# A hybrid attention layer on one core: row scales by PE transposes, x split in pairs, dilated loads one unit ahead

## The chip, the core and the metric

The kernel runs on one core of a Trainium2 chip. TensorE (PE) multiplies matrices into PSUM, whose eight banks per partition all are in use here; VectorE (DVE), ScalarE (ACT) and GpSimd (POOL) work on tiles in SBUF; the queue of SyncE (SP) issues every DMA of this program. Each engine and the queue run their instructions in the order in which the program has them: an instruction that waits holds up all behind it. The metric is the device time in microseconds, the median of several runs.

## What is computed

One decoder layer on x (2048 rows of 1024): an RMSNorm, one input projection, two attention mixers with eight heads of 64 each, a SiLU gate on each, an output projection, and x added. Cut to what matters:

```python
hdn = rmsnorm(x, norm_gain)
q_a, k_a, v_a, g_a, q_b, k_b, v_b, g_b = split(hdn @ w_in)
q_a = rope(rmsnorm(q_a, q_norm_a), pos)      # k_a, q_b, k_b likewise, per head
o_a = banded_attention(q_a, k_a, v_a, 127, sinks) * silu(g_a)
o_b = dilated_attention(q_b, k_b, v_b) * silu(g_b)   # windows (128,1), (512,4), (2048,16)
x = x + concat([o_a, o_b]) @ w_out
```

Mixer A sees 128 keys back and shares each key head among four query heads. Mixer B merges three patterns, weighted by their softmax denominators.

## The kernel before

All matrices are float32. To keep their precision, a factor is split into a high part (`xh`, `wh`, rounded to the PE's format) and the rest (`xl`, `wl`), and every product is three matmuls (`mm3`, L238): high by high, high by low, low by high. `x_split` makes the parts of x: ACT copies `xh` (L154), POOL or DVE subtracts (L156).

The work is cut into eight stages: four B stages (two heads of mixer B each), two A stages (four heads of mixer A each) and two output stages O (half of the output columns each). A stage walks over four blocks `sb` of 512 rows, a block over two halves `hf` of 256 rows. `proj` does a half: two tiles of 128 rows for q, k and v (24 matmuls of 384 columns each), then one gate (B) or two (A) of 24 matmuls with 256 columns, transposed, so that a row's scale lies along the free axis there. The RMSNorm of x isn't applied to x but afterwards: `rst` holds 1/rms of each row as a column (for v and q, k), and `RB` holds half of it as a row, the same in all 128 partitions, for the gate (L317). In the first stage `squares` and `rstd` work the row sums out: for the first two halves from x with a matmul against ones (L198), for the others from `xn`, a second copy of x in row order (L204, L205). `rstd` writes the scales to DRAM as single values (`rsr<-rss`, L213), and every half of every B and A stage loads them back in a broadcast (`RB<-rsr`, L270).

`norm_rope` and `norm_split` make the heads' norm and rotation: POOL raises the mean square to the power -1/2 (`fac`, L182), DVE multiplies (L433), ACT and POOL split (L442 to L445); `qk_transposes` turns the result by PE, through the PSUM bank `tq`. Results of the attention's second product (PV) go through the bank `po`. Both names have one bank; `pj`, `sc` and `pt` have two each.

The attention is cut into units of four steps (scores, transposes, PV, after). Units of the window pattern follow in the same stage (`units_B`, `units_A`); the dilated patterns need all rows, so q, k and v of a B stage are spilled to DRAM and `units_D` loads them again in the stage after it (`cq`, `ck`, `cl`, `cv`). `advance` does one step between two chunks of the projection, as far as a running sum of estimated costs allows; up to three units are in flight. `final` (A) and the end of `after` (D) load a row of softmax factors in a broadcast (`Rb`, one buffer) and multiply on POOL. At the end the Tile framework's scheduler sets the order on each engine and puts in the waits. The profile calls buffers by the names in the code; `in_` marks an input.

Of the kernel before, what the change touches and what calls it, by code (L numbers as in the profile page):

```python
# [21 lines left out]
XB = 3  # L22
# [10 lines left out]
def hybrid_layer(ctx, tc, xT, xn, x, wB, wA, wO, ng, gains, sinks, rot, masks, ident, out):  # L33
# [57 lines left out]
    rs_row = [dram([512], f"rsr{sb}") for sb in range(4)]  # L91
# [58 lines left out]
    def x_split(si, hf, g):  # L150
        f = XS.pop((si, hf, g))
        h = xp.tile([128, 4, 256], F32R, name="xh", bufs=3)
        l = xp.tile([128, 4, 256], F32R, name="xl", bufs=XB)
        nc.scalar.activation(h, f, AF.Copy)  # L154
        eng = nc.gpsimd if g == 0 or hf >= 6 else nc.vector
        eng.tensor_tensor(l, f, f32(h), op=OP.subtract)  # L156
        XG[si, hf, g] = (h, l)
        if si == 0 and hf < 2:
            squares(f, g)

    def first_half():
        for g in range(2):
            f = xp.tile([128, 4, 256], F32, name="xs")
            h = xp.tile([128, 4, 256], F32R, name="xh", bufs=3)
            l = xp.tile([128, 4, 256], F32R, name="xl", bufs=XB)
            for c in range(4):
                nc.sync.dma_start(f[:, c], xT[0][:, 4 * g + c, :])
                W[0][2](4 * g + c, lambda: (nc.scalar.activation(h[:, c], f[:, c], AF.Copy),
                                            nc.vector.tensor_tensor(l[:, c], f[:, c], f32(h[:, c]), op=OP.subtract)))
            XG[0, 0, g] = (h, l)  # L170
            XS[0, 0, g] = f
        for g in range(2):
            squares(XS.pop((0, 0, g)), g)
# [10 lines left out]
    def squares(f, g):  # L184
        sq = wk.tile([128, 4, 256], F32, name="P")
        if g == 0:
            SQ.append(wk.tile([128, 2, 256], F32, name="o1c", bufs=1))
        nc.scalar.activation(sq, f, AF.Square)
        nc.vector.tensor_tensor(sq[:, 0:2], sq[:, 0:2], sq[:, 2:4], op=OP.add)
        nc.vector.tensor_tensor(SQ[-1][:, g], sq[:, 0], sq[:, 1], op=OP.add)  # L190

    def rstd(i0, n):
        ss = wk.tile([128, 4], F32, name="rss")[:, :n]
        if i0 < 4:
            p = ps.tile([128, 2], F32, name="tq")
            for t in range(2):
                for g in range(2):
                    nc.tensor.matmul(p[:, t:t + 1], SQ[-1][:, g, 128 * t:128 * t + 128], one, start=g == 0, stop=g == 1,  # L198
                                     skip_group_check=True)
        else:  # L200
            p = ss
            for i in range(n):
# [794 lines left out]
```

## Time and profile before

| | |
|---|---|
| median of 3 runs | 1323.74 us (1321.75 to 1323.76) |
| profiled execution: its time, and its span from first to last instruction | 1318.66 us, 1316.9 us |
| mean granted clock of TensorE in it | 0.949 |
| busy: PE, DVE, ACT, POOL | 1189.3, 877.2, 821.3, 657.0 us |
| moved by DMA | 228.31 MB, 173 GB/s on average |

The profile is of one execution. A row of a group gives the line, engine and operation, output and inputs, the count, then the busy time, the mean of one instruction in ns, and the idle time just before these instructions with what ended it. "PEclk" is the share of TensorE's full clock that was granted. Matmuls overlap one another, so the mean duration of one is longer than the distance from one to the next. A wait row reads: engine, its output and line, what it waited for, then us in total, times, and the longest.

### The profile page before, as it was taken

The numbers are of one execution on the slowest core, as the hardware profiler recorded it, in microseconds if no ns is written. First come the engines' busy times: TensorE is split into PE (matmuls) and PEld (weight loads), VectorE is DVE, ScalarE is ACT, GpSimd is POOL, SyncE is SP. The second block draws the span as 40 slices with busy tenths as digits, with TensorE's granted clock in tenths as the row PEclk, the third lists the DMA queues.
The fourth block names the chain that finished last, engine by engine and source line by source line (L and its number), as shares of the span: only waits on it lengthen the run. The fifth ranks groups of instructions, "written<-read, shape, count | busy, mean of one in ns | idle before, by whom it ended". The sixth has DMA issues, their size and how long they took to land.

```text
span 1316.9 us, 25065 instructions
## 1 busy us (share of the span) xinstructions
PE 1189.3 (90%) x8264; PEld 1153.3 (88%) x8264; DVE 877.2 (67%) x2280; ACT 821.3 (62%) x2280; POOL 657.0 (50%) x706
## 2 busy tenths in 40 slices
PE   7587788989999899798988999998799989999899
PEld 6586788989889798797988898998799979999898
DVE  6344476867977688766877788898688878632221
ACT  5446567867867687676766776787567757522210
POOL 5564544366553655545565446574445563233122
PEclk8798989989989899998999999999899999999999
DMA  8366578877768776786856864544333214556462
GB/s 253 101 178 170 150 226 202 229 208 200 201 193 252 203 212 179 187 243 183 223 151 211 213 179 147 156 137 141 108 98 97 93 54 142 183 185 214 156 192 89
DMA packets 195729, 228.31 MB, mean 173 GB/s; under 512 B 28560, under 2 KB 140944, under 8 KB 195600
## 3 DMA queue, kind: packets, MB, share of 16 engines
q1 hardware_dynamic: 195600, 226.71, 59.6%
q8 instruction: 66, 1.08, 0.4%
q14 instruction: 63, 0.52, 0.1%
HBM read 171.78 MB, written 54.86 MB: 172 GB/s over the span
## 4 chain that ended last, share of the span: by engine, by line
PE 50%; DMA 20%; DVE 13%; ACT 7%; POOL 4%; issue 4%; SPq 1%; POOLq 0%; DVEq 0%; ACTq 0%
PE pj L238 35%; DMA rsr<-rss 3%; DVE G L322 3%; DVE t L433 2%; PE po L830 2%; DMA Rb<-rD 2%; DMA stg<-in_wB 2%; DMA xs<-in_xT 2%; PE po L629 2%; DMA stg<-in_wO 2%; POOL fac L182 1%; PE pt L703 1%; PE sc L574 1%; PE po L719 1%; DMA stg<-in_wA 1%
## 5 line engine op out<-in xcount | busy, mean ns | idle before, releaser
L238 PE MATMUL pj<-wh,xh 128*128 128x384 f32 (+1 forms) x1008 | 339.4, 338 | 32.4 <-DVE gz L317 23.5
L238 PE MATMUL pj<-wh,xl 128*128 128x384 f32 (+1 forms) x1008 | 338.0, 337 | 7.4 <-DVE xl L156 7.4
L238 PE MATMUL pj<-wl,xh 128*128 128x384 f32 (+1 forms) x1008 | 339.0, 336 | 0.0
L156 POOL TENSOR_TENSOR xl<-xs,xh 128x1024 fp32r<-128x1024 f32 x79 | 191.7, 2429 | 164.1 <-ACT xh L154 163.9
L238 PEld LDWEIGHTS pj<-wh,xh 128*128 128x128 f32 x1008 | 197.2, 196 | 36.5 <-DVE gz L317 25.5
L154 ACT ACTIVATE xh<-xs 128x1024 fp32r<-128x1024 f32 x126 | 133.0, 1056 | 152.7 <-PE pj L238 99.7
L238 PEld LDWEIGHTS pj<-wh,xl 128*128 128x128 f32 x1008 | 197.6, 196 | 9.2 <-DVE xl L156 8.2
L238 PEld LDWEIGHTS pj<-wl,xh 128*128 128x128 f32 x1008 | 197.4, 196 | 1.6 <-DVE wl L104 0.4
L558 DVE TENSOR_TENSOR ptl<-pt,pth 128x512 fp32r<-128x512 f32 (+3 forms) x232 | 141.3, 618 | 31.0 <-ACT pth L557 28.4
L238 PE MATMUL pj<-xh,wgh 128*128 128x256 f32 x496 | 147.4, 297 | 5.1 <-DVE V L300 4.8
L557 ACT ACTIVATE pth<-pt 128x512 fp32r<-128x512 f32 (+3 forms) x232 | 123.0, 543 | 40.4 <-PE pt L816 11.3
L238 PE MATMUL pj<-xh,wgl 128*128 128x256 f32 x496 | 145.1, 292 | 0.0
L238 PE MATMUL pj<-xl,wgh 128*128 128x256 f32 x496 | 145.0, 292 | 0.0
L420 POOL TENSOR_TENSOR t<-t,t 128x256 f32<-128x256 f32 (+1 forms) x96 | 77.4, 806 | 69.7 <-DVE t L411 41.3
L322 DVE SCALAR_TENSOR_TENSOR G<-gz 128x128 f32<-128x128 f32 x128 | 95.3, 783 | 24.1 <-ACT gz L319 23.6
L433 DVE TENSOR_TENSOR t<-t,fac 128x256 f32<-128x256 f32 (+1 forms) x96 | 79.4, 845 | 39.6 <-POOL fac L182 36.9
L238 PEld LDWEIGHTS pj<-xh,wgh 128*128 128x128 f32 x496 | 98.3, 198 | 6.8 <-ACT wh L103 3.4
L238 PEld LDWEIGHTS pj<-xl,wgh 128*128 128x128 f32 x496 | 98.1, 198 | 0.4
L238 PEld LDWEIGHTS pj<-xh,wgl 128*128 128x128 f32 x496 | 98.1, 198 | 0.2
L795 ACT ACTIVATE P<-P,scD 128x256 f32<-128x256 f32 (+3 forms) x128 | 71.6, 561 | 30.9 <-DVE scD L794 29.9
L182 POOL TENSOR_TENSOR fac<-un,mhalf 128x8 f32<-128x8 f32 (+1 forms) x48 | 85.1, 1773 | 2.3
L444 POOL TENSOR_TENSOR hl<-t,hl 128x128 fp32r<-128x128 f32 (+1 forms) x96 | 62.1, 647 | 47.7 <-ACT hl L442 47.6
(185 smaller groups left out, 3064.4 us busy)
## 6 DMA issues: line engine op xcount, KB each, us to landing
xs<-in_xT SPq DMA_DIRECT2D x94, 512.0 KB
xs<-mx SPq DMA_DIRECT2D x32, 512.0 KB
vd<-V SPq DMA_DIRECT2D x64, 128.0 KB
qd<-Q SPq DMA_DIRECT2D x32, 256.0 KB
TT<-tab SPq DMA_DIRECT2D x32, 256.0 KB
cv<-vd SPq DMA_DIRECT2D x32, 256.0 KB
cq<-qd SPq DMA_DIRECT2D x32, 256.0 KB
ck<-kd SPq DMA_DIRECT2D x64, 128.0 KB
```

Of the source, the lines that this page charges most:

```text
L154: nc.scalar.activation(h, f, AF.Copy)
L156: eng.tensor_tensor(l, f, f32(h), op=OP.subtract)
L182: nc.gpsimd.tensor_tensor(y, u, mhalf.to_broadcast([128, n]), op=OP.pow)
L238: nc.tensor.matmul(o, a, b, start=first and n == 0, stop=last and n == 2, skip_group_check=True)
L322: nc.vector.scalar_tensor_tensor(G[si, sb][gc][:, :, 2 * half + j, :], e[:, js].rearrange("p (r u) -> p r u", r=4), 1.0, z[:, js].rearrang ...
L420: nc.gpsimd.tensor_tensor(t1[:, :n], t1[:, :n], t2[:, :n], op=OP.add)
L433: nc.vector.tensor_tensor(t1v, t1v, fac[:, tt, :, None].to_broadcast([128, nh, 64]), op=OP.mult)
L444: nc.gpsimd.tensor_tensor(lo, t1v[:, :nq], f32(hi), op=OP.subtract)
L557: nc.scalar.activation(hi, pt, AF.Copy)
L558: nc.vector.tensor_tensor(lo, pt, f32(hi), op=OP.subtract)
L629: nc.tensor.matmul(po[:, o:o + 256], a, b, start=n_ == 0, stop=n_ == len(seq) - 1, skip_group_check=True)
L795: nc.scalar.activation(pd, pd, AF.Exp, bias=nb, scale=-1.0, accum_out=l)
```

## The change

It has six parts.

1. The row scales of stage one: `rstd` is called for every half, one half ahead, from the loaded x; `xn` isn't read any more. `rb_make` transposes `rst`, spread over 128 columns, on PE, and ACT copies the result to `RB`. One row of it is written to DRAM for the later stages, which load it a half ahead (`rb_load`).
2. `xh` and `xl` are tiles of two chunks instead of four, six buffers each; the third and fourth pair are split in the middle of the last gate.
3. The gate writes its first product into `G` itself, and forms the result there in one instruction instead of two. The rope table is loaded into its place `TT` and multiplied there.
4. `norm_factors` (POOL) comes before the gate's matmuls and `norm_split` after the gate; the transposes of a half (`deferred`) come in the second tile of the next half instead of the first.
5. The loads of a dilated unit are a step of their own, issued when the unit before it starts. The last products of A and D are put into a list `late`, each due after a number of unit steps, and their loads are issued two or three steps before.
6. `tq` and `po` become one name with two buffers; `Q` and its copy `qc` have two buffers each.

The places where the order moves. First SP's queue in stage one, around the third and fourth half: before, the scales' writes (L213), the broadcasts (L270), and tables and x behind them.

```order
L213 DMA rsr_93<-rss 128x2x1
L304 DMA vd_326<-V 4x32x256
L270 DMA RB<-rsr_93 128x256
L304 DMA vd_326<-V 4x32x256
L147 DMA xs<-in_xT 128x1024
L213 DMA rsr_94<-rss 128x4x1
L270 DMA RB<-rsr_94 128x256
L388 DMA tab_2_476<-TT 128x512
L382 DMA gz<-in_rot 128x256
```

And now (`xs` is x, `tab` the rope tables kept for later stages, `vd` the spilled v):

```order
L392 DMA TT<-in_rot 128x4x64
L214 DMA rsr_93<-RB 1x256
L398 DMA tab_1_321<-TT 128x512
L148 DMA xs<-in_xT 128x1024
L398 DMA tab_2_503<-TT 128x512
L314 DMA vd_350<-V 4x32x256
L214 DMA rsr_94<-RB 1x256
```

No load of this stage waits for a write of the scales any more; the writes that are left stand for stage two. Next DVE in the fourth B stage, fourth half, around the gate's first product (L317, now L331); `t` is the rotated q and k, `xl` the low part of x, `ptl` that of the probabilities. Before:

```order
L156 TENSOR_TENSOR xl<-xs,xh 128x1024
L433 TENSOR_TENSOR t_7998<-t_7998,fac 128x256
L558 TENSOR_TENSOR ptl<-pt,pth 128x384
L433 TENSOR_TENSOR t_8035<-t_8035,fac 128x256
L317 TENSOR_TENSOR gz<-pj,RB 128x256
L558 TENSOR_TENSOR ptl<-pt,pth 128x512
L322 SCALAR_TENSOR_TENSOR G<-gz 128x4x32 x2
```

And now:

```order
L157 TENSOR_TENSOR xl<-xs,xh 128x512 x2
L331 TENSOR_TENSOR G<-pj,RB 128x2x4x32
L446 TENSOR_TENSOR t_8241<-t_8241,fac 128x256
L446 TENSOR_TENSOR t_8303<-t_8303,fac 128x256
L335 SCALAR_TENSOR_TENSOR G<-gz,G 128x4x64
```

The products with `fac` have moved from ahead of the gate's first product to behind it. Last POOL at the same place; `osum`, `o1c` and `Rb` belong to the end of a dilated unit. Before:

```order
L874 TENSOR_TENSOR osum<-osum,Rb 128x512
L875 TENSOR_TENSOR o1c<-o1c,Rb 128x512
L428 TENSOR_TENSOR un<-un,eps_84 128x8
L420 TENSOR_TENSOR t_8035<-t_8035,t_8036 128x256
L876 TENSOR_TENSOR osum<-osum,o1c 128x512
L182 TENSOR_TENSOR fac<-un,mhalf 128x8
```

And now:

```order
L899 TENSOR_TENSOR o1c<-o1c,Rb 128x512
L478 CAST qc<-Q 128x8x32
L457 TENSOR_TENSOR hl<-t_7874,hl 128x128
L430 TENSOR_TENSOR t_8241<-t_8241,t_8242 128x256
L458 TENSOR_TENSOR hl<-t_7874,hl 128x128
L457 TENSOR_TENSOR hl<-t_7965,hl 128x128
L458 TENSOR_TENSOR hl<-t_7965,hl 128x128
L904 TENSOR_TENSOR osum<-osum,Rb 128x512
L436 TENSOR_TENSOR un<-un,eps_84 128x8
L905 TENSOR_TENSOR osum<-osum,o1c 128x512
L430 TENSOR_TENSOR t_8303<-t_8303,t_8304 128x256
L182 TENSOR_TENSOR fac<-un,mhalf 128x8
```

The two products with `Rb`, which stood side by side ahead of `fac`, are apart by six other instructions.

The diff, cut to its core:

```diff
-XB = 3
+XB = 6
+QB = {"Q": 2, "qc": 2}
...
-    rs_row = [dram([512], f"rsr{sb}") for sb in range(4)]
+    rs_row = [dram([256], f"rsr{hf}") for hf in range(8)]
...
     def x_split(si, hf, g):
-        f = XS.pop((si, hf, g))
-        h = xp.tile([128, 4, 256], F32R, name="xh", bufs=3)
-        l = xp.tile([128, 4, 256], F32R, name="xl", bufs=XB)
+        f = XS[si, hf, g // 2][:, 2 * (g % 2):2 * (g % 2) + 2]
+        h = xp.tile([128, 2, 256], F32R, name="xh", bufs=XB)
+        l = xp.tile([128, 2, 256], F32R, name="xl", bufs=XB)
         nc.scalar.activation(h, f, AF.Copy)
-        eng = nc.gpsimd if g == 0 or hf >= 6 else nc.vector
+        eng = nc.gpsimd if g < 2 or hf >= 6 else nc.vector
         eng.tensor_tensor(l, f, f32(h), op=OP.subtract)
...
-    def rstd(i0, n):
-        ss = wk.tile([128, 4], F32, name="rss")[:, :n]
-        if i0 < 4:
...
-        else:
-            for i in range(n):
-                t = wk.tile([128, 1024], F32, name="P") if i0 == 4 else xp.tile([128, 1024], F32, name="xs")
-                nc.sync.dma_start(t, xn[(i0 + i) * 128:(i0 + i + 1) * 128, :])
-                nc.scalar.activation(t, t, AF.Square, accum_out=ss[:, i:i + 1])
...
-            nc.sync.dma_start(rs_row[i0 // 4][128 * (i0 % 4):128 * (i0 % 4 + n)].rearrange("(i p) -> p i", p=128), ss)
+    def rb_make(hf):
+        p = ps.tile([128, 2, 128], F32, name="po", bufs=2)
+        for t in range(2):
+            nc.tensor.transpose(p[:, t], rst[:, 2 * hf + t:2 * hf + t + 1].to_broadcast([128, 128]), idf)
+        RBS[0, hf] = wk.tile([128, 256], F32, name="RB")
+        nc.scalar.activation(RBS[0, hf], p.rearrange("p t e -> p (t e)"), AF.Copy, scale=0.5)
+        nc.sync.dma_start(rs_row[hf][None, :], RBS[0, hf][0:1, :])
+
+    def rb_load(si, hf):
+        if si > 0 and STAGES[si][0] != "O":
+            RBS[si, hf] = wk.tile([128, 256], F32, name="RB")
+            nc.sync.dma_start(RBS[si, hf], bcast_row(rs_row[hf], 0, 256))
...
                 if tt == 0 and nx:
-                    x_load(*nx, 0)
                     x_load(*nx, 1)
                     x_split(*nx, 0)
+                    x_split(*nx, 1)
                     if si == hf == 0:
                         late_constants(1)
+                        rb_make(0)
                     rope_tables(*nx)
-                    if si == 0 and sb < 3 and half == 1:
-                        rstd(4 * sb + 4, 4)
-                if tt == 0:
+                    if si == 0 and hf < 7:
+                        for g in range(2):
+                            squares(XS[nx + (g,)], g)
+                    rb_load(*nx)
+                if tt == 1:
+                    if si == 0 and hf < 7:
+                        rstd(hf + 1)
                     while deferred:
                         yield from deferred.pop(0)()
...
-            hls = norm_split(kind, nq, nk, sb, half, t1s, un)
+            fac = norm_factors(nh, sb, half, un)
+            RB = RBS.pop((si, hf))
             for gc in range(ngc):
...
+                    if nx and gc == ngc - 1 and c in (1, 3):
+                        x_split(*nx, 2 + c // 2)
                     yield 330
-                z = wk.tile([128, 256], F32, name="gz", bufs=2)
-                nc.vector.tensor_tensor(z, pg, RB, op=OP.mult)
+                z = G[si, sb][gc][:, :, 2 * half:2 * half + 2, :]
+                nc.vector.tensor_tensor(z.rearrange("p r j u -> p j r u"), jru(pg), jru(RB), op=OP.mult)
                 nc.scalar.activation(e, z, AF.Tanh)
-                for j in range(2):
-                    js = slice(128 * j, 128 * j + 128)
-                    nc.vector.scalar_tensor_tensor(G[si, sb][gc][:, :, 2 * half + j, :],
-                                                   e[:, js].rearrange("p (r u) -> p r u", r=4), 1.0,
-                                                   z[:, js].rearrange("p (r u) -> p r u", r=4), op0=OP.add, op1=OP.mult)
+                nc.vector.scalar_tensor_tensor(z, e, 1.0, z, op0=OP.add, op1=OP.mult)
-            if nx:
-                x_split(*nx, 1)
-                if si == hf == 0:
-                    rstd(2, 2)
+            hls = norm_split(kind, nq, nk, t1s, fac)
+            if si == 0 and hf < 7:
+                rb_make(hf + 1)
...
-                pt = ps.tile([128, 4, 128], F32R, name="tq")
+                pt = ps.tile([128, 4, 128], F32R, name="po", bufs=2)
...
         def after():
             rows(p)
-            final(p)
+            late.append([5, lambda: final(p)])
...
+                def first():
+                    rb = bcast(0)
+                    late.append([3, lambda: second(rb)])
+
+                def second(rb):
+                    nc.gpsimd.tensor_tensor(o1, o1, rb, op=OP.mult)
+                    rb = bcast(1)
+                    late.append([3, lambda: third(rb)])
...
     def advance():
+        tick()
         if not todo:
             if pending:
+                for unit in pending[:2]:
+                    if callable(unit[-1]):
+                        unit.pop()()
                 pipe.append([pending.pop(0), 0])
```

`tick` counts every entry of `late` down by one and runs those that are due.

More of the change, by code (lines that the diff above doesn't have):

```diff
@@ new lines, in squares, with rstd @@
+        for j in range(2):
+            nc.scalar.activation(sq[j], f[:, 2 * j:2 * j + 2], AF.Square)
+        nc.vector.tensor_tensor(sq[0], sq[0], sq[1], op=OP.add)
+        nc.vector.tensor_tensor(SQ[-1][:, g], sq[0][:, 0], sq[0][:, 1], op=OP.add)
+    def rstd(hf):
+        ss = wk.tile([128, 2], F32, name="rss")
+        p = ps.tile([128, 2], F32, name="po", bufs=2)
+        for t in range(2):
+            for g in range(2):
+                nc.tensor.matmul(p[:, t:t + 1], SQ[-1][:, g, 128 * t:128 * t + 128], one, start=g == 0, stop=g == 1,
+                                 skip_group_check=True)
+        c = slice(2 * hf, 2 * hf + 2)
@@ L256, in proj @@
             return
-        Q[si, sb] = [st.tile([128, 2, 4, 128], F32R, name="Q", bufs=3) for _ in range(nq // 2)]
-        qc = st.tile([128, 2, 4, 4, 32], F32R, name="Q", bufs=3) if kind == "B" else None
+        Q[si, sb] = [st.tile([128, 2, 4, 128], F32R, name=nm, bufs=QB[nm]) for nm in ("Q", "qc")]
         K[si, sb] = (st.tile([128, nk, 4, 5, 32], F32R, name="KK"), KLZ[(4 * si + sb) % 2])
@@ L266, in proj @@
             nx = next_half(si, hf)
-            xg = [XG.pop((si, hf, g)) for g in range(2)]
+            xg = [XG.pop((si, hf, g)) for g in range(4)]
             TC, TS = TB.pop((si, hf))
-            RB = wk.tile([128, 256], F32, name="RB", bufs=1)
-            nc.sync.dma_start(RB, bcast_row(rs_row[sb], half * 256, 256))
+            if nx:
+                x_load(*nx, 0)
             t1s = []
@@ L366, in hybrid_layer @@
     deferred = []
+    late = []
     tabs = {}
@@ L429, in norm_split @@
         rsqrt(fac.rearrange("p a h -> p (a h)"), u.rearrange("p a h -> p (a h)"), 2 * nh)
+        return fac
+    def norm_split(kind, nq, nk, t1s, fac):
+        nh = nq + nk
+        n = nh * 64
         hls = []
@@ L912, in hybrid_layer @@
     first_half()
-    rstd(0, 2)
+    rstd(0)
     late_constants(0)
@@ L924, in hybrid_layer @@
         own = {"B": 4 * 2900, "A": 4 * 2600, "O": 0}[kind] if n else 0
-        total = left + sum(c for u in pending for _, c in u) + own
+        total = left + sum(st_[1] for u in pending for st_ in u if not callable(st_)) + own
         done = pr = 0.0
```

160 lines of the change are left out of this document (81 added, 79 removed).

## The prediction

> **What bounds it now.** The page comes first.
>
> ```profile
> span 1316.9 us, 25065 instructions
> PE 1189.3 (90%) x8264; PEld 1153.3 (88%) x8264; DVE 877.2 (67%) x2280; ACT 821.3 (62%) x2280; POOL 657.0 (50%) x706
> PEclk8798989989989899998999999999899999999999
> PE 50%; DMA 20%; DVE 13%; ACT 7%; POOL 4%; issue 4%; SPq 1%; POOLq 0%; DVEq 0%; ACTq 0%
> ```
>
> TensorE (PE) is busy 1189 of 1317 us, so at most 128 us are plain idle time; the digits of its granted clock, with sevens and eights among the nines of the left half and hardly any at the right, say that more is lost by slow matmuls. Half of the chain that ended last is PE, a fifth is DMA. Where that is, a table by stage tells. The windows are the start of the second half-block of projection stage one (25 us), the starts of the stages after it (second to fourth B stage, two A stages), and the first output stage; columns are length, busy time and instructions of PE, of its weight loads, of DVE, ACT and POOL, the granted clock, DMA share and GB/s.
>
> ```profile
> 25.00:185.00 160.00, 119.45 (x708) 115.92 (x708) 71.50 (x191) 85.39 (x223) 88.46 (x119) 0.83 0.57 165
> 185.00:349.00 164.00, 155.10 (x1058) 150.45 (x1057) 125.41 (x336) 121.63 (x346) 86.70 (x101) 0.97 0.76 211
> 349.00:523.00 174.00, 160.35 (x1082) 154.91 (x1081) 131.13 (x344) 128.30 (x360) 93.43 (x107) 0.95 0.73 208
> 523.00:705.00 182.00, 164.78 (x1086) 158.63 (x1087) 132.76 (x344) 126.37 (x358) 99.66 (x112) 0.93 0.72 198
> 705.00:918.00 213.00, 197.29 (x1375) 188.26 (x1374) 179.20 (x489) 153.59 (x457) 124.14 (x134) 0.98 0.58 167
> 918.00:1106.00 188.00, 173.73 (x1224) 169.76 (x1223) 150.40 (x412) 125.67 (x383) 97.20 (x92) 0.96 0.32 96
> 1106.00:1213.00 107.00, 106.99 (x889) 106.18 (x888) 47.67 (x102) 43.45 (x97) 36.35 (x22) 1.00 0.59 184
> ```
>
> Stage one needs 160 us for 708 matmuls, 0.226 us each, with PE idle 40.6 us at a clock of 0.83. The next three B stages take 0.155, 0.161 and 0.168 us for one. The output stage at 1106 runs 889 matmuls at clock 1.00 without idle time, 0.120 us each. So stage one is the slow place, and the chain inside it names the cause:
>
> ```profile
> by line: DMA rsr<-rss 28.1%; DMA xs<-in_xn 9.4%; DMA xs<-in_xT 7.8%; issue 6.7%; DVE G L322 4.3%; DMA P<-in_xn 3.4%; PE pj L238 3.4%; DMA stg<-in_wB 2.8%; POOL fac L182 2.7%; DMA gz<-in_rot 2.5%; ACT xs L205 2.4%; DMA RB<-rsr 2.4%; POOL TT
> ...
> 38.38 5.47 DMA P<-in_xn
> ...
> 60.18 9.98 DMA rsr<-rss
> ...
> 71.10 4.02 DMA gz<-in_rot
> ```
>
> The write of the row scales to DRAM in single 4-byte values (rsr<-rss) holds 28.1% of these 160 us, 45 us in five writes, one of them 9.98 us. Loads of the second copy of x (in_xn, into xs and P) hold 12.8%, 20.5 us. The row scales come back as the broadcast RB, which the gate's first DVE product (L317) needs, and PE's accumulators come free only behind that product. PE's waits, first in stage one, then in the rest of the span:
>
> ```profile
> PE pj L238 <- DVE gz L317: 11.2, 2, 6.3
> PE tq L461 <- POOL hl L444: 9.0, 1, 9.0
> ```
>
> ```profile
> PE pj L238 <- DVE gz L317: 12.3, 6, 4.1
> PE pt L603 <- DVE ptl L558: 6.9, 2, 6.2
> PE po L629 <- DVE osum L552: 6.5, 3, 3.7
> PE sc L789 <- DMA ck<-kd: 6.0, 3, 3.4
> PE sc L574 <- ACT KK L478: 4.8, 1, 4.8
> PE pj L238 <- DVE xl L156: 4.8, 2, 4.2
> PE po L830 <- DVE ptl L558: 4.0, 1, 4.0
> PE po L629 <- DVE ptl L558: 3.9, 3, 1.7
> PE tq L470 <- ACT klz L479: 3.4, 1, 3.4
> ```
>
> These nine rows hold 52.6 us. Behind several of them stands one event, seen at 606 to 619 us on DVE and POOL (start, duration, instruction, idle time before it and its releaser):
>
> ```profile
> 612.10 1.28 POOL L875 TENSOR_TENSOR o1c<-o1c,Rb 128x512 f32<-128x512 f32 x1 [4.44 <-DMA Rb<-rD]
> 615.42 1.65 POOL L182 TENSOR_TENSOR fac<-un,mhalf 128x8 f32<-128x8 f32 x1
> ```
>
> ```profile
> 617.10 1.48 DVE L433 TENSOR_TENSOR t<-t,fac 128x256 f32<-128x256 f32 x1 [7.19 <-POOL fac L182]
> ```
>
> POOL waits 4.44 us for the broadcast Rb, so fac is computed late; DVE stands 7.19 us before L433, and the probability split that PE wants, and the gate product, queue behind it. Over the span DVE loses this much there, and POOL this much to the two Rb loads of a dilated unit:
>
> ```profile
> DVE t L433 <- POOL fac L182: 36.9, 10, 8.1
> ```
>
> ```profile
> POOL o1c L875 <- DMA Rb<-rD: 44.9, 12, 9.3
> POOL osum L874 <- DMA Rb<-rD: 33.8, 6, 11.0
> ```
>
> **The change, part by part.** *Row scales in stage one.* Removed from its chain are the five 4-byte writes, the eight RB loads of that stage and the twelve loads of in_xn. In their place stand, a half ahead, 32 half-width ACT squares for 16 full-width ones, 32 DVE additions for eight, eight pairs of PE transposes with an ACT copy each, eight 1-KB writes on SP, and 24 more of the L198 column sums. What stage one costs without the round trips I read from its neighbours, which have the same projections and no round trip on their chain: 708 matmuls at 0.155 to 0.168 us are 110 to 119 us. I take the slowest neighbour, 119, because stage one has none of the cheap transposes of dilated units in its mix: 41 us saved. The ends are 50 us (fastest neighbour) and 20 us (only the waits on gz and hl go, 11.2 + 9.0). The price of the new PE work:
>
> ```profile
> 17.43 0.73 PE L198 MATMUL tq<-one,o1c 128*128 128x1 f32 x6
> ```
>
> Six such records take 0.73 us, 0.122 each. The 24 column sums are 48 records (each is recorded twice), with 16 transposes 64 records, 7.8 us; half falls into idle time that is left, so 4 us on the path (0 to 8). The new transposes also wait at the head of PE's queue for POOL's power of the row sums, with the next projection's matmuls behind them; late by one POOL subtraction of x (2.43 us, row below) in each of eight halves that is 19 us, which the 20-us end covers. I count none, since the column sum and the transpose of a half stand some 30 projection matmuls apart, 3.6 us at 0.120. Stage one: -41 + 4 = -37 us.
>
> *x in pairs of chunks.* ACT copies 252 halves for 126 wholes, and POOL and DVE subtract twice as often at half the width:
>
> ```profile
> L154 ACT ACTIVATE xh<-xs 128x1024 fp32r<-128x1024 f32 x126 | 133.0, 1056 | 152.7 <-PE pj L238 99.7 <-DMA xs<-in_xT 36.0 <-PE pt L238 8.4
> L557 ACT ACTIVATE pth<-pt 128x512 fp32r<-128x512 f32 x144 | 84.1, 593 | 19.5 <-PE pt L703 11.3 <-PE pt L609 3.8 <-PE po L719 2.5
> L156 POOL TENSOR_TENSOR xl<-xs,xh 128x1024 fp32r<-128x1024 f32 x79 | 191.7, 2429 | 164.1 <-ACT xh L154 163.9
> L672 POOL TENSOR_TENSOR o1c<-osum,Rb 128x512 f32<-128x512 f32 x16 | 21.2, 1327 | 48.5 <-DMA Rb<-rA 38.2 <-DMA stg<-in_wO 9.7 <-POOL hl L445 0.7
> L322 DVE SCALAR_TENSOR_TENSOR G<-gz 128x128 f32<-128x128 f32 x128 | 95.3, 783 | 24.1 <-ACT gz L319 23.6
> ```
>
> By the 512-wide copy, 252 x 0.593 = 149 for 133 us on ACT; by the 512-wide POOL product, 158 x 1.327 = 210 for 192 us on POOL. That is +16 and +18 us on engines that idle 496 and 660 us, so nothing on the path by itself; the cover is that idle time, and in stage one POOL, busy 88 of 160 us, would be busy some 90 of 123. What it buys: the second half of x, before split in one piece once the gate's fourth chunk is done, is now split after its second and its fourth, which bears on the row DVE xl (4.8 us).
>
> *Gate.* Two 128-wide products become one 256-wide one: 64 instructions for 128 at 0.783 us. If one costs as much as one now, DVE saves 50 us of 877; if it costs two, nothing. It shortens the gate's tail, which no PE wait names; I count nothing.
>
> *Order of the norm.* fac is issued ahead of the gate's matmuls, and L433's products behind the gate's first product, so what waited behind L433 on DVE (gz, ptl) no longer does; in exchange the q/k transposes run one tile later, at the second projection tile of the next half, and attention units start that much later. The late list cuts POOL's final products into steps of two or three unit steps after their loads are issued, so the 78.7 us of the two Rb rows mostly go, and SP no longer stands before Rb until rD has landed. *Dilated loads* go out a unit ahead: the ck row, 6.0 us. *Shared banks:* transposes and PV take turns in two banks instead of one each: the osum row (6.5) and the KK and klz rows (8.2). Behind the dilated loads on SP's queue stand x and weight loads; they have a whole half-block of lead.
>
> All nine rows of the rest of the span are thus touched: 52.6 us is one end, and 0 the other if each wait only moves to the next item of an in-order queue. I take the middle, 26 us, nearer to neither, as the example at 617 us shows both: the wait goes, and DVE still has the same products to do.
>
> The sum: -37 - 26 = -63 us. The profiled execution took 1318.66 us with a span of 1316.9; the median of the three runs, 1323.74, is 5.1 above it. So 1255.7 for a profiled run and 1260.7 for the median; I say 1261.
>
> The clock is a reserve that this sum does not hold. In the five windows from 185 to 1106 the shares short of 1.00 times the lengths are 4.9 + 8.7 + 12.7 + 4.3 + 7.5 = 38 us. The Trainium skill, "TensorE: Matmul & The Clock Gate" (Part 1: The HAM clock gate), says that the array's clock falls to half after an idle window of about 3.4 us and comes back after a busy one. The windows agree in kind: 0.83 where PE waits 9.0 us at a time, 1.00 where it never waits. By that rule half of the waits would take half of the 38 us with them, 19 us, and the sum would be 1242.
>
> **The rivals.** *Stage one alone (1287).* The waits after 185 us move but do not shrink, 1323.74 - 37. For it: 496 us of ACT idle time and 440 of DVE did not prevent them. Against it: the event at 617 us has a named cause that goes.
>
> *Both at their good ends (1228).* Stage one at the fastest neighbour's rate (-46 with the added PE work) and the other waits nearly all gone (-50). For it: the lost clock above, which goes with the waits.
>
> *The rope tables become late (1298).* The table is now loaded straight into TT in 256-byte runs, and read and written in place by POOL. The load took 4.02 us at 71.10 in 1-KB runs; the 4-byte write at 60.18, 9.98. Nearer to the first, but if it costs the second, eight halves pay 6 us each, 48, and eat stage one's 37. It decides once load and four POOL products outlast a half (some 15 us), since the load is issued a half ahead; that speaks against it. The Trainium skill, "DMA: Bandwidth & Descriptors" (Specifications), sets 512 B as the least transfer for full rate and has shorter ones read, modified and written; by that rule this load is slower than before, and the rival gets its chance. The runs of before agree only at 4 bytes.
>
> *Slower (1343): the shared banks hold up PE.* 304 uses (96 PV, 160 q/k transposes, 48 small ones) take turns in two banks, and every use waits until the last but one is read out. A PV result is read by two instructions:
>
> ```profile
> L550 ACT ACTIVATE ob<-po 64x512 f32<-64x512 f32 x64 | 38.0, 594 | 12.0 <-PE po L629 7.0 <-PE po L830 3.1 <-ACT pth L557 0.9
> L554 DVE TENSOR_TENSOR osum<-po,ob 64x512 f32<-64x512 f32 x32 | 21.7, 680 | 2.5 <-ACT ob L550 1.8
> ```
>
> That is 0.594 + 0.680 = 1.27 us; 96 times 122 us. If half of the PV results stopped PE for that long, the gain of 63 would be gone; at two thirds, 82 us, the time is 1343. For it: transposes never stood behind PV before. Against it: with a single bank PV waited on osum just three times, 6.5 us.
>
> **How the numbers follow.** My case 0.50 (about 1240 to 1280), stage one alone 0.17, both good ends 0.17, late tables 0.08, slower 0.08. The range takes in 1225 (a little under the good ends) to 1300 (late tables); beyond lie the slower rival and some tail of the good one, 0.15 together. Faster by over 0.2%, about what a measurement of this kernel can tell from no change: 0.92; of the banks' 0.08, 0.06 is slower and 0.02 within 0.2%.
>
> **What would show it.** Right: no rsr<-rss on the chain; stage two starts near 148 us instead of 185, with a clock over 0.93 in stage one; the wait of the norm product on fac under 12 us of 36.9; POOL's waits on Rb under 25 us of 78.7. Wrong: new PE waits on po (banks), DVE waits on TT (tables), stage one past 165 us, or the rows gz and ptl at their old sums.

## The result, and the profile after

The changed kernel takes 1268.9 us in the median (1265.6 to 1271.7), the kernel before, run beside it, 1322.7: a ratio of 0.9594, 95% interval 0.9561 to 0.9627, 53.8 us less. The profiled execution has a span of 1269.9 us for 1316.9; it was the longest of its four, and that of before (1318.66 us) shorter than every run behind its median, so the profiles differ by 47.0 us where the medians differ by 53.8. The page of after, its span, busy times and granted clock:

```profile
span 1269.9 us, 25442 instructions
PE 1179.8 (93%) x8328; PEld 1143.5 (90%) x8328; DVE 867.5 (68%) x2288; ACT 837.1 (66%) x2418; POOL 685.3 (54%) x788
PEclk9899989999999899898998999999899999999999
```

The chain that ended last can't be followed back to stage one here, so that the write of the scales is off it is read from PE's waits below. PE has 64 matmuls more and is busy for 9.5 us less. The sevens and eights that stood at the start of its clock are now eights and nines. By stage (first half-block left out, then the start of each stage as before: three more B stages, two A stages, the first output stage; length, busy time and instructions of PE, its weight loads, DVE, ACT and POOL, granted clock, DMA share, GB/s):

```profile
23.00:157.00 134.00, 119.67 (x780) 116.00 (x781) 90.14 (x213) 88.45 (x247) 99.83 (x132) 0.92 0.48 139
157.00:326.00 169.00, 151.29 (x1042) 147.04 (x1040) 120.88 (x329) 123.31 (x360) 89.91 (x111) 0.98 0.74 209
326.00:501.00 175.00, 160.80 (x1073) 154.73 (x1074) 125.54 (x341) 127.56 (x373) 96.56 (x117) 0.95 0.73 205
501.00:672.00 171.00, 161.47 (x1087) 156.57 (x1085) 128.70 (x349) 128.95 (x378) 97.43 (x119) 0.95 0.74 211
672.00:871.00 199.00, 189.91 (x1346) 183.33 (x1346) 167.44 (x460) 147.04 (x446) 129.18 (x143) 0.98 0.61 176
871.00:1058.00 187.00, 179.68 (x1274) 172.53 (x1273) 147.27 (x426) 137.45 (x431) 104.11 (x105) 0.98 0.32 99
1058.00:1167.00 109.00, 107.12 (x888) 106.13 (x887) 49.40 (x106) 46.46 (x116) 38.31 (x31) 1.00 0.59 184
```

Stage two starts at 156.7 us for 185.3: 28.6 us of the 47.0 by which the span is shorter. The rest, 18.4 us, lies in the stages behind; of these the two A stages (213 and 189 us in before) now take 199 and 187. PE's waits in stage one, then in the rest (us in total, times, longest):

```profile
PE pj L244 <- DVE V L310: 4.7, 2, 4.3
PE sc L244 <- POOL xl L157: 4.5, 2, 2.3
PE po L211 <- POOL rst L182: 3.1, 2, 2.9
PE pj L244 <- ACT xh L155: 2.6, 1, 2.6
PE po L474 <- ACT RB L213: 1.1, 1, 1.1
```

```profile
PE po L474 <- POOL hl L457: 7.9, 7, 2.0
PE pj L244 <- DVE V L310: 7.2, 7, 2.5
PE po L498 <- ACT KK L477: 6.4, 2, 5.5
PE pj L244 <- ACT xh L155: 4.1, 1, 4.1
PE po L474 <- DVE osum L570: 3.7, 1, 3.7
PE pt L828 <- DVE ptl L574: 2.8, 2, 1.5
PE pt L619 <- DVE ptl L574: 2.7, 1, 2.7
PE pj L244 <- ACT wh L101: 2.2, 2, 2.0
PE po L484 <- DVE osum L740: 2.0, 1, 2.0
```

The waits on the gate's product, 11.2 and 12.3 us before, are down to 0.8 us. In stage one only small rows are left. In the rest the waits have moved to the q/k transposes (L474, L498) and to V, in smaller pieces; only one of these rows stands for the x split (ACT xh). Where the prediction expected DVE and POOL to stop waiting, they have not:

```profile
DVE t L446 <- POOL fac L182: 30.1, 13, 5.7
```

```profile
POOL o1c L899 <- DMA Rb<-rD: 55.1, 13, 7.6
POOL osum L904 <- DMA Rb<-rD: 39.7, 13, 6.7
```

DVE still waits 30.1 us on fac, and POOL waits 94.8 us for the broadcasts of a dilated unit where it waited 78.7. The costs of what was added (line, count, busy time, mean ns of one, idle time before it):

```profile
L155 ACT ACTIVATE xh<-xs 128x512 fp32r<-128x512 f32 x252 | 153.5, 627 | 115.8 <-PE pj L244 98.8 <-DMA xs<-in_xT 8.3 <-issue 4.3
L157 POOL TENSOR_TENSOR xl<-xs,xh 128x512 fp32r<-128x512 f32 x158 | 213.7, 1365 | 143.8 <-ACT xh L155 139.1 <-DMA TT<-tab 2.2
L335 DVE SCALAR_TENSOR_TENSOR G<-gz,G 128x256 f32<-128x256 f32 x64 | 47.5, 742 | 9.3 <-ACT gz L334 9.1
L198 PE MATMUL po<-one,o1c 128*128 128x1 f32 x64 | 8.7, 248 | 0.0
L211 PE MATMUL po<-idf,rst 128*128 128x128 f32 x16 | 3.4, 297 | 3.1 <-POOL rst L182 3.1
L395 POOL TENSOR_TENSOR TT<-TT,gt 128x128 f32<-128x128 f32 x64 | 35.1, 570 | 34.4 <-DMA TT<-in_rot 34.4
```

### The profile page after: what moved, and what is told of

The parts are those of the page before. It is cut to its first block, busy times and chain, and to the rows that moved or that the text cites. A ratio compares the mean times of both kernels' runs of the same rounds, so it can differ in the third digit from the quotient of the medians.

```text
span 1269.9 us, 25442 instructions
## 1 busy us (share of the span) xinstructions
PE 1179.8 (93%) x8328; PEld 1143.5 (90%) x8328; DVE 867.5 (68%) x2288; ACT 837.1 (66%) x2418; POOL 685.3 (54%) x788
## 5 line engine op out<-in xcount | busy, mean ns | idle before, releaser
L244 PE MATMUL pj<-wh,xh 128*128 128x384 f32 (+1 forms) x1008 | 334.1, 334 | 18.6 <-ACT xh L155 6.7
L244 PE MATMUL pj<-wl,xh 128*128 128x384 f32 (+1 forms) x1008 | 334.9, 332 | 1.4 <-DVE wl L102 0.8
L244 PE MATMUL pj<-wh,xl 128*128 128x384 f32 (+1 forms) x1008 | 331.9, 331 | 1.1 <-POOL xl L157 0.8
L157 POOL TENSOR_TENSOR xl<-xs,xh 128x512 fp32r<-128x512 f32 x158 | 213.7, 1365 | 143.8 <-ACT xh L155 139.1
L155 ACT ACTIVATE xh<-xs 128x512 fp32r<-128x512 f32 x252 | 153.5, 627 | 115.8 <-PE pj L244 98.8
L244 PEld LDWEIGHTS pj<-wl,xh 128*128 128x128 f32 x1008 | 194.6, 193 | 3.6 <-DVE wl L102 1.1
L244 PEld LDWEIGHTS pj<-wh,xl 128*128 128x128 f32 x1008 | 194.4, 193 | 3.5 <-DVE xl L157 1.3
L446 DVE TENSOR_TENSOR t<-t,fac 128x256 f32<-128x256 f32 (+1 forms) x96 | 76.9, 815 | 33.0 <-POOL fac L182 30.1
L814 ACT ACTIVATE P<-P,scD 128x128 f32<-128x128 f32 (+3 forms) x128 | 71.6, 560 | 40.5 <-DVE scD L813 39.6
L157 DVE TENSOR_TENSOR xl<-xs,xh 128x512 fp32r<-128x512 f32 x94 | 79.8, 859 | 20.2 <-ACT xh L155 19.8
L599 ACT ACTIVATE P<-P,scA 128x256 f32<-128x256 f32 (+1 forms) x128 | 63.1, 495 | 23.4 <-DVE scA L598 23.0
```

The costliest lines, as they stand in the source:

```text
L244: nc.tensor.matmul(o, a, b, start=first and n == 0, stop=last and n == 2, skip_group_check=True)
L446: nc.vector.tensor_tensor(t1v, t1v, fac[:, tt, :, None].to_broadcast([128, nh, 64]), op=OP.mult)
L599: nc.scalar.activation(pd, pd, AF.Exp, bias=nb[i], scale=-1.0, accum_out=l[i])
L814: nc.scalar.activation(pd, pd, AF.Exp, bias=nb, scale=-1.0, accum_out=l)
```

## The experiments

Lengths of stages are what tells most here. They are taken from the first projection matmul of a stage to that of the next; "B" is the sum of the second to fourth stage, "A" of the two A stages, "O" of the two output stages, all in the one profiled execution of the kernel. The ratio is to the runs of before on the same chip. All in us.

| kernel | median | ratio (95%) | stage one | B | A | O |
|---|---|---|---|---|---|---|
| before | 1322.7 | 1 | 179.5 | 519.4 | 401.6 | 210.6 |
| changed | 1268.9 | 0.9594 (0.9561 to 0.9627) | 151.1 | 515.7 | 386.0 | 211.6 |
| rows_only | 1289.2 | 0.9736 (0.9705 to 0.9768) | 162.5 | 528.5 | 378.5 | 210.3 |
| no_rows | 1300.2 | 0.9819 (0.9774 to 0.9864) | 179.9 | 519.6 | 380.6 | 212.5 |
| no_late | 1285.2 | 0.9703 (0.9666 to 0.9741) | 149.3 | 524.0 | 387.9 | 211.6 |
| norm_before | 1269.7 | 0.9584 (0.9542 to 0.9625) | 148.8 | 518.3 | 381.4 | 213.5 |
| pace_before | 1321.7 | 0.9995 (0.9965 to 1.0025) | 180.7 | 522.8 | 396.3 | 214.9 |
| pace2_before | 1309.1 | 0.9904 (0.9878 to 0.9929) | 181.6 | 527.2 | 378.9 | 215.9 |
| pace_after | 1273.6 | 0.9637 (0.9622 to 0.9652) | 149.2 | 517.0 | 388.4 | 213.3 |
| banks_apart | 1274.2 | 0.9649 (0.9623 to 0.9675) | 154.3 | 522.9 | 381.8 | 214.4 |
| x_whole | 1262.5 | 0.9549 (0.9529 to 0.9568) | 143.3 | 509.9 | 383.5 | 216.9 |
| xw_gate | 1273.9 | 0.9654 (0.9601 to 0.9706) | 145.1 | 514.7 | 394.3 | 211.3 |
| xw_defer0 | 1273.0 | 0.9644 (0.9599 to 0.9688) | 153.2 | 507.1 | 384.7 | 217.2 |
| xw_no_ahead | 1267.2 | 0.9611 (0.9561 to 0.9662) | 145.6 | 516.7 | 388.5 | 216.0 |

**rows_only: the row scales alone, on the kernel before.** Part 1 of the change and nothing else; `RB` keeps one buffer, the small results go through `tq`, and the later stages load `RB` where they did.

```diff
-    rs_row = [dram([512], f"rsr{sb}") for sb in range(4)]
+    rs_row = [dram([256], f"rsr{hf}") for hf in range(8)]
...
+    def rb_make(hf):
+        p = ps.tile([128, 2, 128], F32, name="tq")
```

> The kernel before with the row scales of stage one alone done in the new way (rstd per half from the loaded x, spread by PE transposes; no xn, no 4-byte writes); from stage two on everything as before. Theory S (stage one's 29 us, start of stage two at 157 instead of 185, come from the lost round trips alone): 1294 us, within 5, stage two starting at 155 to 160, and the stages behind it as long as before. Rival J (the gain needs the other parts too, the earlier x and the moved norm): 1305 or more, stage two not before 168.

**no_rows: the changed kernel without that part**, the row scales made, written and loaded as before (the edit is the reverse of the one above).

> The changed kernel with the row scales of stage one made and spread in the old way (xn, 4-byte writes, RB loaded at the start of a half into one buffer), all other parts kept. Theory S: 1298 us, stage two starting near 185, the PE waits behind it as in the changed kernel, so that what the other parts give (some 18 us) stays. Rival J: 1285 or less, since the other parts shorten stage one too; stage two starting before 178.

Measured: 1289.2 and 1300.2, where before took 1323.8 on that chip: the row scales alone give 34.6 us, the other parts alone 23.6. no_rows came as theory S had it; rows_only fits neither theory, faster than S by the time, with stage two at 168.0 us as J had it. The stages say more. In stage one the row scales alone give 17 us, the other parts alone nothing, both together 28. And rows_only is 23 us shorter in the A stages, whose code it does not touch. The window of stage one in rows_only:

```profile
23.00:168.00 145.00, 122.87 (x769) 116.29 (x769) 94.98 (x213) 88.12 (x233) 97.79 (x121) 0.88 0.44 129
```

It is idle for 22 us (145.00 less 122.87) at a clock of 0.88, against 14 us at 0.92 in the window of after: the round trips are gone, but something else holds PE up, which the other parts remove. Its longest wait there is at the transposes of q and k, which in this kernel still stand in the first tile and go through the single bank `tq`:

```profile
PE tq L470 <- ACT ck L187: 5.4, 1, 5.4
```

One more thing changed. PE's waits on the gate's product, 23.5 us over the span of before, are 1.7 us in rows_only, although its norm order is the old one; in two other orders of the code before they stay at 18.6 and 19.1 (pace_before and pace2_before below). Behind stage one they are 12.3 in before, 1.7 in rows_only and 3.1 in no_rows. So either side of the change ends them there, and the norm's order isn't needed for it; why the row scales of stage one do it in later stages, the runs do not show.

**no_late: the changed kernel without the list `late`**; products and loads stand together again, at the end of the unit.

```diff
-            late.append([5, lambda: final(p)])
+            final(p)
...
-                    late.append([3, lambda: second(rb)])
...
-                late.append([2, first])
+                nc.gpsimd.tensor_tensor(o2, o2, bcast(1), op=OP.mult)
+                nc.gpsimd.tensor_tensor(o1, o1, bcast(0), op=OP.mult)
```

> The changed kernel without the late list: the ends of A and D units load Rb and multiply in one go, as before. Theory E (the list gives nothing, since POOL's waits on Rb are 95 us in the changed kernel and were 79 before): 1269 us, within 5. Rival P (the prediction's claim, the list frees POOL and through fac DVE): 1280 or more, with DVE's waits on fac at 36 us or more instead of 30.

**norm_before: the norm's DVE products ahead of the gate again**, behind POOL's factors, which stay where the change put them.

```diff
-            hls = norm_split(kind, nq, nk, t1s, fac)
...
+            hls = norm_split(kind, nq, nk, t1s, norm_factors(nh, sb, half, un))
```

> The changed kernel with norm_split called before the gate's matmuls again (its products with fac ahead of the gate's first product on DVE); transposes stay in the second tile. Theory N (this move is what took the gate product out from behind fac): 1277 us or more, PE waits on the gate product (L331 or its line here) back at 8 us or more. Rival R (the wait only changes its victim): 1269 within 5, with fewer PE waits on the low parts of q and k (hl) than the 9.0 us of the changed kernel.

Measured: no_late 1285.2, 16 us over the changed kernel, 8.4 of it in the profiled execution and there in the B stages (+8.3). By the time theory P holds: 16 us is more than re-sorting did to the changed code below (5 us), and to the old (11). But the 8.3 us of the B stages are no more than the B stages of before differ between executions (see below), so where the loss lies isn't shown. norm_before 1269.7, no change, and PE's waits on the gate's product stay at 1.0 us: the order of norm and gate is not needed to end them. DVE and POOL in no_late:

```profile
DVE t L446 <- POOL fac L182: 38.4, 14, 6.6
```

```profile
POOL o1c L895 <- DMA Rb<-rD: 31.7, 13, 7.1
POOL osum L894 <- DMA Rb<-rD: 23.5, 6, 6.9
```

Without the list POOL waits less for Rb (55.2 us for 94.8), and yet the kernel is slower. So POOL's idle time before Rb was no measure of the cost. DVE's wait on fac is none either: it is 38.4 us here for 30.1, but 36.4 in pace_after, which keeps the list and takes 1273.6. What the list did not end is the event itself. In the changed kernel, on POOL and on DVE:

```profile
414.48 1.29 POOL L904 TENSOR_TENSOR osum<-osum,Rb 128x512 f32<-128x512 f32 x1 [5.83 <-DMA Rb<-rD]
418.50 1.65 POOL L182 TENSOR_TENSOR fac<-un,mhalf 128x8 f32<-128x8 f32 x1
```

```profile
420.18 0.94 DVE L446 TENSOR_TENSOR t<-t,fac 128x256 f32<-128x256 f32 x1 [5.66 <-POOL fac L182]
```

POOL ends a wait of 5.83 us for Rb, finishes the unit and only then works out fac, for which DVE has stood 5.66 us. How much of POOL's 94.8 us stands before fac in this way was not measured, and by what path the list gains its time stays open.

**pace_before, pace2_before, pace_after: the same code in another order.** The A stages of rows_only had gained 23 us without a cause in their code. One pair of numbers, the estimate of a stage's own cost by which `advance` spreads the attention steps, re-sorts the program and changes no operation:

```diff
-        own = {"B": 4 * 2900, "A": 4 * 2600, "O": 0}[kind] if n else 0
+        own = {"B": 4 * 2800, "A": 4 * 2500, "O": 0}[kind] if n else 0
```

pace2_before has 2700 and 2400.

> The kernel before with one pair of numbers changed that has no part in the change: the estimate of a stage's own cost in advance(), from 2900 and 2600 to 2800 and 2500 a chunk group, so attention steps fall between slightly other projection chunks. Theory C (the order around an edit is a draw: any edit re-sorts the waits): single B and A stages move by 5 to 15 us either way with no part changed, the median by up to 10. Rival D (stages repeat): each stage within 3 us of 164, 174, 182, 213 and 189, median within 4 us of 1324. If D holds, the 10 and 13 us that the A stages of the run with the row scales alone gained belong to the row scales; if C holds, no part may be given a gain under 10 us from one run.

> The changed kernel with the same change of pace. Theory C: single stages 5 to 15 us off 169, 175, 172, 199 and 187, median 1260 to 1280. Rival D: each stage within 3 us, median 1265 to 1273.

> The kernel before with the estimate of a stage's own cost set to 2700 and 2400. The first change of pace (2800 and 2500) left the order on DVE word for word and moved twelve rows on PE, so its equal stages proved nothing; this one re-sorts PE from the middle of its list on (third B stage and all after it) and leaves the first stages alone. Theory C (draw): the two A stages, 213 and 189 us before, lose or gain 8 us or more with no part of the change made, as they did by 10 and 13 us with the row scales of stage one alone; median 1300 to 1330. Rival D (the A stages are slow for a cause that one of the parts removes): both within 4 us, median 1318 to 1328.

Measured: by the traces pace_before runs PE in the old order up to 785 us, DVE and ACT up to 896, so that its A stages are re-sorted in part. (The expectation of pace2_before says of it that DVE's order stayed word for word; the traces show otherwise from 899 us on.) Its stages came within 5 us, the A stages together at 396.3 for 401.6, and its median within 2, nearly as rival D had it. pace_after differs from the changed kernel from 712 us on: within 3 us by stage, 5 in the median, again nearly rival D. pace2_before differs on PE from 681 us on, in the fourth B stage. It takes 1309.1, 1% less than before, and its A stages 378.9 us for 401.6; the second one alone is 17 us shorter. So theory C holds in one of three re-sortings: the 401.6 of before is the long end of what orders of this code give. Four orders of the old code in the A stages (before, pace_before, rows_only, pace2_before) gave 402, 396, 379 and 379; the changed code gave 386 and 388.

These runs also show what repeats. With PE, DVE, ACT and POOL in the same order, or nearly, stage one took 179.5, 180.7 and 181.6 us in before, pace_before and pace2_before (179.9 in no_rows, with the same row scales), and 151.1 and 149.2 in after and pace_after. The B stages took 519.4, 522.8 and 527.2, and 515.7 and 517.0. Differences under some 2 us in stage one, or some 8 in the B stages, are therefore not to be read.

**banks_apart: transposes in `tq`, PV in `po` again**, one bank each.

```diff
-                pt = ps.tile([128, 4, 128], F32R, name="po", bufs=2)
+                pt = ps.tile([128, 4, 128], F32R, name="tq")
...
-            po = ps.tile([128, 512], F32, name="po", bufs=2)
+            po = ps.tile([128, 512], F32, name="po")
```

> The changed kernel with the two shared banks given apart again, one for transposes and small results, one for PV. Theory S (sharing gains the waits on osum, KK and klz, 15 us in the page of before, by half): 1273 to 1280, and those rows come back. Rival B (sharing costs as much as it gains, PE waits on hl and osum through the shared bank): 1265 to 1271. Third: sharing holds PE up, 1255 to 1264.

Measured: 1274.2, 5 us more, within what an order may do. By the time that is theory S, but not all of its rows came back: PE's wait on osum through `po` is 0.5 us, and that at L498 on KK, 5.4 here, is 6.4 in the changed kernel. In stage one, where orders moved little (148.8 to 151.1 us in four kernels with the changed code there), it is 3 to 5 us longer, in an execution that was the longest of its four (1280.6 us). PE's waits in the bank of the transposes, the first of them for 2.5 us in stage one, the others there only:

```profile
PE tq L498 <- ACT KK L477: 5.4, 5, 2.5
PE tq L198 <- ACT RB L213: 5.3, 3, 2.6
PE tq L211 <- POOL rst L182: 4.3, 1, 4.3
```

The second row is new: with one bank the column sums (L198) wait until the row broadcast before them has been copied out, 5.3 us. So sharing is not seen to cost anything, and seems to save a few microseconds in stage one.

**x_whole: x split in fours again**, the second half in one piece after the gate's fourth chunk.

```diff
-XB = 6
+XB = 3
...
-        h = xp.tile([128, 2, 256], F32R, name="xh", bufs=XB)
+        h = xp.tile([128, 4, 256], F32R, name="xh", bufs=XB)
...
-                    if nx and gc == ngc - 1 and c in (1, 3):
-                        x_split(*nx, 2 + c // 2)
+                    if nx and gc == ngc - 1 and c == 3:
+                        x_split(*nx, 1)
```

> The changed kernel with x split in fours again (126 ACT copies and as many subtractions as before, the third and fourth pair in one piece after the gate's fourth chunk). Theory P (pairs bring x in time): PE waits on xl and xh rise by 5 to 12 us, most of it in stage one, 1274 to 1281. Rival Q (the halves cost as much on POOL and DVE as they bring): 1266 to 1272, with ACT 20 us and POOL 15 to 20 us less busy.

Measured: 1262.5, which neither theory had: faster than the changed kernel, and the fastest version that was run. The two 95% intervals overlap a little (0.9568 and 0.9561), so that is probable by the time alone; by stage one it is plain: 143.3 us, and 145.1 and 145.6 in the two kernels below that share its x split and its order of transposes, against 148.8 to 151.1 in the four with pairs. The halves (first projection matmul of the fifth to the eighth half, then of stage two) show where: 97.4, 121.3, 140.5, 156.7 with pairs, 96.9, 116.5, 133.0, 148.5 without. The stretch of the fifth and sixth half in after and in x_whole:

```profile
97.40:140.50 43.10, 37.30 (x258) 36.01 (x257) 27.73 (x70) 30.55 (x86) 28.02 (x39) 0.96 0.40 113
```

```profile
96.90:133.00 36.10, 34.32 (x252) 33.87 (x251) 22.59 (x59) 28.01 (x75) 27.44 (x35) 1.00 0.48 137
```

PE is idle 5.8 us for 1.8 and runs at a clock of 0.96 for 1.00. One wait carries most of the idle time. On SP, ACT and DVE of after (start, duration, instruction, idle time before it and its releaser):

```profile
102.46 0.36 SPq L148 DMA_DIRECT2D xs<-in_xT  x1
...
106.28 0.45 SPq L148 DMA_DIRECT2D xs<-in_xT  x1
```

```profile
112.17 0.63 ACT L189 ACTIVATE cq<-xs 128x512 f32<-128x512 f32 x1 [1.89 <-DMA xs<-in_xT]
...
114.21 0.35 ACT L410 ACTIVATE V<-pj,rst 128x128 fp32r<-128x128 f32 x1
```

```profile
115.27 0.34 DVE L310 SCALAR_TENSOR_TENSOR V<-pj,rst,V 128x128 fp32r<-128x128 f32 x1
```

The second load of x is issued at 106.28 us, behind five stores that follow the first one; ACT's square (L189), now a half ahead, waits for it until 112.17, V's first half (L410) queues behind it, DVE finishes V at 115.6, and PE has waited 4.29 us for it (the 4.3 of the row on V in stage one). In x_whole that load goes out at 103.54, and PE waits 1.8 us there. The wait goes with the pairs: the longest one on V is 3.4 to 4.3 us in the four kernels with pairs, 1.8 to 2.6 in the three with fours. Whether the pairs themselves make it late, or only the order that comes with them, these runs do not separate: ACT's whole wait for x in stage one is about the same in both, 22.2 and 20.4 us. Nor are the engines busier with pairs. Stage one of after and of x_whole, without the first half:

```profile
23.00:156.70 133.70, 119.37 (x779) 115.70 (x780) 89.92 (x212) 88.16 (x246) 99.53 (x132) 0.92 0.48 138
```

```profile
23.00:148.50 125.50, 115.04 (x775) 112.87 (x776) 88.19 (x204) 86.75 (x232) 98.97 (x122) 0.93 0.51 148
```

DVE, ACT and POOL are busy within 2 us of each other; what differs is when they run.

**xw_gate, xw_defer0, xw_no_ahead: three parts undone on x_whole**: the gate's two 128-wide products, the transposes in the first tile of the next half, the dilated loads at their own step.

```diff
-                nc.vector.scalar_tensor_tensor(z, e, 1.0, z, op0=OP.add, op1=OP.mult)
+                for j in range(2):
+                    js = slice(128 * j, 128 * j + 128)
+                    nc.vector.scalar_tensor_tensor(G[si, sb][gc][:, :, 2 * half + j, :],
...
-                if tt == 1:
+                if tt == 0:
                     while deferred:
...
             def scores():
+                load()
...
-            return [(scores, 1194), (transposes, 1090), (pv, 1194), (after, 60), load]
+            return [(scores, 1194), (transposes, 1090), (pv, 1194), (after, 60)]
```

> The changed kernel with x split in fours (1262 us), and with the gate as before: its product into a tile of its own, the result in two 128-wide instructions. My step counted the gate at nothing on the path; DVE should do some 40 us more. Step right: 1258 to 1267. Rival: DVE's longer list delays the probability split and the norm products, 1268 to 1280.

> The changed kernel with x split in fours (1262 us), and with the q/k transposes of a half back in the first tile of the next half. Theory N: the later tile lets the norm and the splits run beside projection matmuls, so taking it back brings PE waits on hl (the splits of the rotated q and k): 1268 to 1280, most of it in the B stages. Rival: attention starts earlier and the waits are the same: 1255 to 1265.

> The changed kernel with x split in fours (1262 us), and with a dilated unit's loads issued at its own scores step again. By my step the wait on ck comes back, 6 us and what queues behind it: 1266 to 1274, all of it in the second to fifth stage. Rival: the loads have lead enough through the units in flight, 1259 to 1265.

Measured: 1273.9, 1273.0 and 1267.2. xw_gate's 11 us lie in the A stages (+10.8), where an order alone moved 23, so they prove nothing on the gate, though the time is the rival's. On DVE its old form takes 71.6 us for the 128 products, 24 more than the 64 of after:

```profile
L333 DVE SCALAR_TENSOR_TENSOR G<-gz 128x128 f32<-128x128 f32 x128 | 71.6, 598 | 13.3 <-ACT gz L330 12.1 <-POOL osum L685 1.0
```

xw_defer0 is told by stage one: 153.2 us for 143.3 to 145.6, 8 to 10 longer, with its window and the wait of PE at the transposes of the row scales:

```profile
23.00:158.80 135.80, 119.48 (x779) 114.45 (x780) 91.69 (x206) 86.61 (x232) 97.37 (x122) 0.91 0.47 138
```

```profile
PE po L210 <- POOL rst L181: 5.1, 4, 2.5
```

PE waits there 5.1 us on POOL's power, a row that x_whole doesn't have. So the transposes one tile later belong to what freed stage one, which the prediction had put under the rest. Theory N had the time (1268 to 1280) but not the place: it expected most of the loss in the B stages, which are not longer (507.1 us for 509.9). xw_no_ahead is 5 us slower in the median, 13 in the profiled span, but the wait on ck did not come back: 2.1 us, for 0.9 in x_whole and 6.0 in before.

```profile
PE sc L806 <- DMA ck<-kd: 2.1, 2, 1.1
```

Nor is there a larger wait on a dilated load, so the difference is open; it has the size of a change of order.

## Why the prediction was right, and where not

1261 was forecast, 1268.9 came, inside the range: the likeliest case. The forecast gain was 63 us, the measured one 53.8 by the medians and 47.0 in the profiles, and by the profiles each term of the sum brought some three quarters of its forecast (28.6 of 37, 18.4 of 26).

**Stage one, -37, measured -28.6.** The neighbours' rate as a measure of what stage one costs without round trips held in x_whole: there stage two starts at 148.5 us, where the prediction had near 148. The step that failed is the one that costed the pairs at "nothing on the path by itself". Their sizes were right (ACT 153.5 us for 149 forecast, POOL 213.7 for 210), and POOL and ACT were idle enough on average (POOL was busier than forecast in stage one, 99.8 us of 134 for some 90, but with x in fours it is 99.0); but stage one, from its fifth half on, is 3 to 8 us longer with x in pairs: with x in fours stage two starts at 148.5, 150.4 and 150.9 us in three kernels. The other price, of PE's new work, was right in size: the column sums and transposes take 8.7 + 3.4 us, of which 2.8 were there before, 9.3 for 7.8; how much of it lies on the path wasn't measured. The wait of the transposes on POOL's power, which I did not count, is 3.1 us.

**The gain of stage one is not the row scales' alone.** I took it as theirs; alone they bring 17 us. The transposes in the second tile bring 8 to 10 more (xw_defer0), the shared banks perhaps 3 to 5 (banks_apart), and the pairs, or the order that comes with them, take 3 to 8 back. These figures come from single executions on different bases, and need not add up.

**The rest, -26, measured -18.4: right in size, mostly by luck.** Of the 18.4 us 15.6 lie in the A stages, 3.7 in the B stages, and the output stages lose 1.0. The A stages get as much from a mere change of order, so these 15.6 us are not to be booked to any part. In the B stages, where the list and the norm order work, before and its re-sorted copies take 519 to 527 us, the changed code 516 and 517: 2 to 12 us less, and part of that is scatter. That is what the mechanism can have earned. The late list may carry it (no_late is slower by 16 us); the order of norm and gate carries nothing, and the waits on the gate's product, which I put down to it, end without it. By the example at 617 us I took POOL's idle time before Rb for the cause, and forecast under 25 us there and under 12 on fac. They are 94.8 and 30.1. The step that failed there is that the list would end POOL's wait, and that SP would no longer stand before Rb until rD has landed. It still does, 28.3 us for 35.0. SP's rows before and after:

```profile
SPq L866 <- DMA rD<-rr: 35.0, 12, 4.9
```

```profile
SPq L890 <- DMA rD<-rr: 28.3, 12, 5.1
```

**The clock.** The lost clock in the five windows behind stage one, worked out as in the prediction, is 3.4 + 8.8 + 8.6 + 4.0 + 3.7 = 28.5 us for 38; as the shares have two digits, either sum can be off by 4.5 us. The waits that I counted there went from 52.6 us in nine rows to 39 in the nine largest of after, so both fell by about a quarter. The 19 us of reserve needed half of the waits to go. The Trainium skill, "TensorE: Matmul & The Clock Gate" (Part 1: The HAM clock gate), ties the clock to idle windows of about 3.4 us. The two falls agree with that in kind but do not test it, since only three of the nine rows of after hold a single wait that long (5.5, 4.1 and 3.7 us). In stage one the clock is 0.92, just under the 0.93 I named.

**The rivals.** Stage one alone, 1287: the time speaks against it, the mechanism hardly; without the A stages' 15.6 us the kernel would stand at 1284.5. Late tables: POOL idles 34.4 us before the table's products (L395), 14.2 of it at the start, yet no instruction of DVE waits on TT. In the nine cases where POOL waited, the load in 256-byte runs took 3.3 to 6.0 us from issue to the first product, nearer to the 4.02 of before than to 9.98 (the longest was issued at 40.80, and POOL went on at 46.80). Shared banks slower: ruled out by the time, and banks_apart is not faster. Both good ends: the waits of the rest were reduced, not removed, and stage one did not reach its neighbours' best rate.

## What to carry to other kernels

A stage's neighbours with the same work and without the stall give a good price for the stall; what is bought along with its removal (here x in pairs) has to be priced inside that stage, and not by busy and idle time: with x in pairs and in fours DVE, ACT and POOL are equally busy there, and the stage differs by 3 to 8 us. Nor does an engine's idle time before a wait say what the wait costs: POOL waited less for Rb without the list, and the kernel was slower. Before a stage's gain is booked to an edit that does not touch it, the old code should be run in another order: here that alone was worth 11 us, 1% of the kernel before.

## What the runs showed of the hardware

Half the width costs more than half: the copy on ACT takes 1056 ns for 1024 elements and 627 for 512, the subtraction on POOL 2429 and 1365. On DVE the gate's second product takes 783 ns on average for 128 elements in before, 598 in xw_gate, and 742 for 256 in after: the same operation differs by a third between two kernels, and twice the elements took no longer than the slower of them. Writing the gate's first product through a permuted view costs nothing (L331 413 ns on average, L317 before 416).
